# Other margins for places in scratch, a narrower float32r arena and another order of heads in a one-core decoder step

## The chip, the cores and the metric

The kernel runs on 1 core of one Trainium2 chip, as one launch. The metric is the device time of that launch in microseconds (us), the median of several runs. Five engines work side by side: PE (TensorE, the matmuls, with its weight loads as PEld), DVE (VectorE), ACT (ScalarE), POOL (GpSimd) and SP (SyncE, which here issues every DMA). Each takes its instructions in the order in which the program lists them for it, and an instruction that waits holds back what is behind it on its engine.

## The reference, cut to what matters

One decoder layer runs on 16 meta tokens, a prompt of 256 and 8 samples of 4 tokens, 304 columns in all. The width is 2048.

```python
xn = rms_norm(x, norm_mix)
z = xn @ w_in                                  # RWKV columns | retention columns
o_a, S_a = rwkv7_mixer(z_a, z_prev, S_a0, ...) # 16 heads of 64, a scan over tokens
o_b, S_b = retention_mixer(z_b, S_b0, ...)     # 4 heads of 256, chunks of 128
h = x + concatenate([o_a, o_b]) @ w_out
hn = rms_norm(h, norm_ffn)
h = h + (silu(hn @ w_gate) * (hn @ w_up)) @ w_down     # 2048 -> 5632 -> 2048
```

A last RMS norm gives the outputs; the states of both mixers, for the prompt and for each sample, are outputs too. All of it is float32.

## The kernel before, in words

**The weight stream.** Every large product is done with float32r matmuls on split operands: a 128x512 block of weights comes in by DMA (`wr<-big`), ACT casts it to its high part (`wh`), DVE subtracts to get the low part (`wl`), and PE runs three matmuls for each 128x128 piece: high x high, high x low, low x high (`acc<-xh,wh` and so on). `main` (line 712) walks through `steps()`: the input projection `w_in`, then the output projection in two halves, then gate, up and down of the FFN. Five raw blocks and five split ones are in flight (`WR`, `WS`). SP issues the loads of this stream between all other DMAs, in one queue.

**The order of the input projection.** `sequence()` (line 110) reads `ORDER`: `pN` are the three tiles (k, r, v) of a pair of RWKV heads, `rN` the six tiles (q, k, v) of a retention head, `gN` the two gate tiles of a retention head. A tile is 16 steps of three matmuls. The host packs the weights into `big` in the same order.

**The streams beside it.** Each finished tile starts generators: `pair` (a pair's chunked RWKV scan: LoRA products, `inverse`, `units`, `sample`, `pair_out`), `ret` (a retention head), `gate_jobs`, and later `sample_state` and `held_states`, which update the samples' states. A generator yields where it would wait. Their small matmuls go to PE as `mm`, between those of the main stream. After the output projection (`"hs"`), `sample_state` runs for the eight pairs one after the other (`rest_of(self.later)`): each makes `s0n` (128x512) and loads it on SP, makes `bt` (128x128) and clears it on POOL, fills `bt` and `vx` (128x512) on ACT, multiplies `bt` by `vx` on PE, and adds the product to `s0n`, which is then stored.

**The draft.** `body` (line 1956) builds the program twice. The first build is a draft: `Plan` keeps a modelled clock for each engine (`book`, line 377), and `pick` decides by it which stream goes on next. In the draft every scratch tile has a buffer of its own, so nothing waits for a place. The decisions are logged, and the second build repeats them, so the order of each engine's instructions comes from the draft alone.

**Places in scratch.** In the second build all scratch tiles lie in two arenas, one of float32 and one of float32r (`arena_dt.float` and `arena_dt.float32r` in the profile). Their addresses come from `Room`. During the draft `Room.use` (line 532) notes for each tile its size, the numbers of its first and last instruction, the time `at` of its first use and the time `until` at which its last use is done. What counts as the time of first use is set in `book`: PE's present matmul for PE, the engine's own clock less 400 ns for DVE, ACT and POOL, SP's clock less 8000 ns for SP. POOL's clock moves when POOL does something: a clear of a fresh tile starts in the draft as soon as the clear before it is done.

`Room.pack` (line 561) then takes the tiles one by one in a given order, mostly the largest first. Two tiles whose ranges of instructions overlap may not share an address. For any other tile already placed it works out a margin: the later one's `at` less the earlier one's `until`, cut to 0 if negative. A margin of 2000 ns or more doesn't count as near. Candidates are the lowest address and the ends of near tiles, in order of address; the one with the largest margin is taken, or the first that reaches `gap`; of equal ones the lowest address stays. `place` tries five orders of tiles and falling values of `gap`, and keeps the packing with the least `lack`, the sum of what each tile's margin falls short of 800 ns. The float32r arena is packed first, within `WIDE` = 4288 elements per partition; the float32 arena gets what is left of `ROOM` = 33008.

In the second build a tile that gets another's place waits, by semaphore, until the instructions on the earlier tile are done. If its first instruction is a load, SP waits; if a clear, POOL; otherwise ACT or DVE.

Of the kernel before, what the change touches and what calls it, by code (L numbers as in the profile page):

```python
# [53 lines left out]
RAHEAD = 2  # L54
RSTART = (-1, -1, 6, 5)
RRANK = (20, 21, 22, 2.5)
ORDER = "p0 p1 p2 r0 p3 p4 r1 g0 p5 p6 g1 p7 r2 g2 g3 r3"


PV = {}  # L60
# [22 lines left out]
KEYS = ((0, META, SEQ, 0), (P, P, NP - P, SEQ), (LASTK, 2 * P, T - 2 * P, SEQ + NP - P))  # L83
RMW = SEQ + NP - P + T - 2 * P
ROOM = 33008
WIDE = 4288
FREE, GAPS, TRIES = 800.0, (2000.0, 1000.0, 500.0, 200.0, 50.0, 0.0), 12


# [20 lines left out]
def sequence():  # L110
# [3 lines left out]
    seq = [("in", i) for i in range(3)]  # L114
    for what in ORDER.split():
        h = int(what[1])
# [206 lines left out]
class Plan:  # L323
# [53 lines left out]
    def book(self, eng, what, a, k):  # L377
        self.count += 1
        if not self.draft:
            return  # L380
        aps = [x for x in (*a, *k.values()) if hasattr(x, "shape")]
        out, ins = aps[0], aps[1:]

        at = 0.0
        boxes = [(x.name, self.box(x), x is out) for x in aps if x.name not in self.outside]
        meet = lambda a, b: a[0] < b[1] and b[0] < a[1] and a[2] < b[3] and b[2] < a[3]
        for name, box, writes in boxes:
            for other, done, by, written in self.uses.get(name, ()):
                if (written or writes) and done + 100 > at and not (by == eng == "PE") and meet(box, other):
                    at = max(at, done + (30 if by == eng else 100 if eng == "PE" else 60))  # L390
        n = math.prod(out.shape[1:])
        if eng == "PE":
            done = self.array(what, *a[:3], at) + 170
        elif eng == "SP":
            self.clock[eng] = at = max(self.clock[eng] + 400, at)
            self.dma = max(self.dma, at + 1400) + 4 * out.shape[0] * n / 320
            done = self.dma + 600
        else:
            each = sum(math.prod(x.shape[1:]) == 1 for x in ins) if n > 1 else 0
            if eng == "DVE":  # L400
                big = max(math.prod(x.shape[1:]) for x in aps)
                per = 0.56 if what == "tensor_scalar" and ins[0].name not in self.banks else 1.05
                dur, tail = {"stream_shuffle": (62 + 1.05 * n, 90), "transpose": (95 + 1.02 * n, 80), "tensor_reduce": (40 + 1.8 * big, 85),
                             "tensor_tensor_scan": (65 + 2.1 * n, 85)}.get(what, (62 + per * n + 67 * each, 83))
            elif eng == "ACT":
                dur, tail = 108 + 0.83 * n + 90 * each - 40 * (ins[0].name in self.banks), 94
            else:
                dur, tail = (60 + 0.85 * n, 60) if what == "memset" else (125 + 0.8 * n, 65) if what == "tensor_copy" else (185 + 1.65 * n, 60)
            key = (out.start_partition(), ins[0].start_partition() if ins else 0)
            ready = self.clock[eng]  # L410
            if eng != "POOL" and key != self.part[eng]:
                ready += tail + (25 if eng == "ACT" else 31)
                self.part[eng] = key
            self.started = max(ready, at)
            at = self.share(eng, what, ins, self.started, dur, each) + dur
            self.clock[eng] = at
            done = at + tail
        for x in aps:
            for room in self.rooms.values():
                room.use(x, self.count, self.begun if eng == "PE" else self.clock[eng] - (8000 if eng == "SP" else 400), done)  # L420
        for name in {x.name for x in aps if x.name in self.left}:
            self.left[name] -= 1
            assert self.left[name] >= 0, name
            if not self.left[name]:
                self.free[self.at.pop(name)] = done
        for name, box, writes in boxes:
            uses = self.uses.setdefault(name, [])
            if writes:
                uses[:] = [u for u in uses if not (box[0] <= u[0][0] and u[0][1] <= box[1] and box[2] <= u[0][2]
                                                   and u[0][3] <= box[3])]  # L430
            uses.append((box, done, eng, writes))
        self.end = max(self.end, done + 100)
# [87 lines left out]
class Room:  # L520
# [40 lines left out]
    def pack(self, order, limit, gap):  # L561
        done, places, lack, end = [], [0] * len(self.spans), 0.0, 0
        for i in order:
            size, a, b, at, until = self.spans[i]
            size = -(-size // 8) * 8
            near = []
            for o, n, c, d, s, u in done:
                if a <= d and c <= b:
                    near.append((o, o + n, -1.0))
                else:  # L570
                    free = max(0.0, at - u if d < a else s - until)
                    if free < 2000.0:
                        near.append((o, o + n, free))
            near.sort()
            best = None
            for o in sorted({0, *(e for _, e, _ in near)}):
                if o + size > limit:
                    break
                free = min((f for s, e, f in near if s < o + size and o < e), default=2000.0)
                if free > -1.0 and (best is None or free > best[0]):  # L580
                    best = free, o
                    if free >= gap:
                        break
            if best is None:
                return i
            lack += max(0.0, FREE - best[0])
            places[i] = best[1]
            end = max(end, best[1] + size)
            done.append((best[1], size, a, b, at, until))
        return lack, end, places  # L590
# [1365 lines left out]
def body(tc, I, O):  # L1956
# [5 lines left out]
    Step(tile.TileContext(nc[0]).__enter__(), nc[1], nc[2], ExitStack(), rooms, True, log).build(gam4)  # L1962
    rooms[F32R].place(WIDE)
    rooms[F32].place(ROOM - rooms[F32R].size)
# [24 lines left out]
```

## Time and profile before

| | us |
|---|---|
| median of 3 runs | 1529.55 (1529.4 to 1532.66) |
| the profiled execution | 1529.31 |
| its span, first to last instruction | 1527.4 |
| PE busy | 1496.6 |
| weight loads busy | 1474.8 |
| DVE busy | 1086.4 |
| ACT busy | 884.1 |
| POOL busy | 30.6 |

The profile is of one execution. A line of the timeline has the start and the length of an instruction (several alike are merged, with their count), its engine, its operation, and the tiles as out<-in; in brackets stands how long the engine was idle before it, and who ended that wait. A line of the waits has the sum, the number and the longest. `acc` are the accumulators of the main stream, `mm` the other banks. All scratch tiles appear under the two arenas' names, so a tile is recognized by its shape, its operation and its place in time. Nearly all instructions carry one line number, that of the helper which records them (L318). In time the span divides thus: the input projection up to about 549 us, the output projection from 572, the FFN from some 686 to 1515.

### The profile page before, as it was taken

What the parts mean: (1) busy time and instruction counts of PE and PEld (TensorE: products, weight loads), DVE (VectorE), ACT (ScalarE), POOL (GpSimd) and SP (SyncE); (2) the same over time, 40 slices, a digit from 0 to 9 for tenths busy, and PEclk for the clock granted to TensorE, in tenths of its full rate; (3) what the DMA queues carried; (4) which work ended last, traced back from release to release, by engine and by line L of the source; (5) the groups of instructions that cost most, each with busy time, mean ns of one, the idle gap of its engine ahead of it and who ended that gap; (6) DMA issues with size and microseconds to landing.
All of it is one profiled execution on the core that took longest, in us unless ns stands there. A gap on an engine that the chain in (4) does not pass through costs nothing.

```text
span 1527.4 us, 31997 instructions
## 1 busy us (share of the span) xinstructions
PE 1496.6 (98%) x11438; PEld 1474.8 (97%) x11438; DVE 1086.4 (71%) x2768; ACT 884.1 (58%) x2109; POOL 30.6 (2%) x165
## 2 busy tenths in 40 slices
PE   8999999999999999999999999999999999999997
PEld 8999899999999989998899999999999999999997
DVE  6989888998999758775565656556565656565657
ACT  6786668887876875566644444444444444444445
POOL 1000000000000000000000000000000000000000
PEclk9999999999999999999999999999999999999999
DMA  7654443554444358865665655565655555555563
GB/s 236 178 139 145 157 150 114 172 165 136 128 130 132 103 188 263 301 173 176 210 174 171 173 167 172 169 176 167 173 167 172 173 172 168 173 170 171 171 174 123
DMA packets 138783, 258.57 MB, mean 169 GB/s; under 512 B 16256, under 2 KB 22656, under 8 KB 138624
## 3 DMA queue, kind: packets, MB, share of 16 engines
q1 hardware_dynamic: 138624, 256.52, 55.9%
q8 instruction: 91, 1.49, 0.4%
q14 instruction: 68, 0.56, 0.1%
HBM read 242.18 MB, written 14.28 MB: 168 GB/s over the span
## 4 chain that ended last, share of the span: by engine, by line
PE 92%; DVE 3%; ACT 2%; DMA 1%; issue 1%; SPq 0%; DVEq 0%; ACTq 0%
PE acc L318 82%; PE mm L318 11%; DVE arena_dt.float L318 2%; ACT arena_dt.float L318 1%; DVE wl L318 1%; DMA wr<-big 1%; ACT wh L318 0%; DMA arena_dt.float<-xT 0%; SPq L318 0%; DMA arena_dt.float<-s0r 0%; DVE arena_dt.float32r L318 0%; ACT arena_dt.float32r L318 0%; DVE xl L318 0%; DMA arena_dt.float<-lora 0%; ACT xh L318 0%
## 5 line engine op out<-in xcount | busy, mean ns | idle before, releaser
L318 PE MATMUL acc<-xh,wh 128*128 128x288 f32 (+2 forms) x2592 | 781.7, 302 | 1.2 <-ACT wh L318 1.2
L318 PE MATMUL acc<-xh,wl 128*128 128x288 f32 (+2 forms) x2592 | 764.1, 295 | 0.4 <-DVE wl L318 0.3
L318 PE MATMUL acc<-xl,wh 128*128 128x288 f32 (+2 forms) x2592 | 761.0, 294 | 0.0
L318 ACT CAST wh<-wr 128x512 fp32r<-128x512 f32 (+1 forms) x827 | 504.8, 616 | 355.2 <-PE acc L318 306.0
L318 DVE TENSOR_TENSOR wl<-wr,wh 128x512 fp32r<-128x512 f32 (+1 forms) x827 | 559.6, 685 | 129.8 <-ACT wh L318 126.4
L318 PEld LDWEIGHTS acc<-xh,wh 128*128 128x128 f32 x2592 | 487.2, 188 | 5.9 <-issue 3.6
L318 PEld LDWEIGHTS acc<-xl,wh 128*128 128x128 f32 x2592 | 486.7, 188 | 3.0 <-issue 1.9
L318 PEld LDWEIGHTS acc<-xh,wl 128*128 128x128 f32 x2592 | 485.7, 187 | 1.3 <-DVE wl L318 0.9
L318 PE MATMUL acc<-arena_dt.float32r,wh 128*128 128x288 f32 x1408 | 273.0, 292 | 0.2 <-DVE arena_dt.float L318 0.2
L318 PEld LDWEIGHTS acc<-arena_dt.float32r,wh 128*128 128x128 f32 x1408 | 223.8, 188 | 0.6 <-DVE arena_dt.float L318 0.4
L318 PE MATMUL acc<-arena_dt.float32r,wl 128*128 128x288 f32 x704 | 205.7, 292 | 0.0
L318 DVE TENSOR_TENSOR arena_dt.float<-acc,arena_dt.float 128x288 f32<-128x288 f32 (+4 forms) x181 | 72.7, 419 | 149.9 <-PE acc L318 147.1
L318 PE MATMUL mm<-arena_dt.float 128*128 128x128 f32 (+6 forms) x1120 | 164.0, 300 | 15.3 <-issue 9.0
L318 DVE TENSOR_TENSOR arena_dt.float<-arena_dt.float 128x32 f32<-128x32 f32 (+22 forms) x658 | 159.9, 279 | 14.2 <-ACT arena_dt.float L318 8.8
L318 PEld LDWEIGHTS mm<-arena_dt.float 128*128 128x128 f32 (+1 forms) x1120 | 138.8, 182 | 25.2 <-issue 13.7
L318 DVE TENSOR_TENSOR arena_dt.float<-arena_dt.float,acc 128x288 f32<-128x288 f32 (+1 forms) x210 | 94.5, 451 | 85.9 <-PE acc L318 82.0
L318 ACT ACTIVATE arena_dt.float<-arena_dt.float 128x288 f32<-128x288 f32 (+7 forms) x229 | 97.2, 432 | 99.3 <-DVE arena_dt.float L318 96.9
L318 PEld LDWEIGHTS acc<-arena_dt.float32r,wl 128*128 128x128 f32 x704 | 132.2, 188 | 0.0
L318 ACT COPY arena_dt.float<-mm 64x64 f32<-64x64 f32 (+10 forms) x338 | 94.8, 289 | 59.0 <-PE mm L318 50.6
L318 ACT COPY arena_dt.float<-arena_dt.float 128x32 f32<-128x32 f32 (+8 forms) x267 | 62.3, 283 | 26.1 <-DVE arena_dt.float L318 22.1
L318 ACT CAST arena_dt.float32r<-arena_dt.float 128x288 fp32r<-128x288 f32 (+6 forms) x117 | 49.4, 429 | 48.4 <-DVE arena_dt.float L318 40.2
L318 DVE TENSOR_TENSOR arena_dt.float32r<-arena_dt.float,arena_dt.float32r 128x288 fp32r<-128x288 f32 (+6 forms) x116 | 52.1, 452 | 18.5 <-ACT arena_dt.float32r L318 18.1
(68 smaller groups left out, 573.3 us busy)
## 6 DMA issues: line engine op xcount, KB each, us to landing
wr<-big SPq DMA_DIRECT2D x823, 256.0 KB, 2.8
arena_dt.float<-s0r SPq DMA_DIRECT2D x24, 512.0 KB, 5.6
out_rts<-arena_dt.float SPq DMA_DIRECT2D x16, 512.0 KB, 4.3
arena_dt.float<-s0w SPq DMA_DIRECT2D x16, 256.0 KB, 2.9
arena_dt.float<-xT SPq DMA_DIRECT2D x4, 576.0 KB, 6.3
arena_dt.float<-lora SPq DMA_DIRECT2D x16, 128.0 KB, 2.5
out_rws<-arena_dt.float SPq DMA_DIRECT2D x8, 256.0 KB, 3.2
out_y<-arena_dt.float SPq DMA_DIRECT2D x7, 288.0 KB, 2.4
```

The lines of the kernel that those rows point to most:

```text
L318: return self._plan.keep(f(*a, **k))
```

## The change

`ORDER` is another: `g0` comes right after `r0` (before: after `r1`), and `p7` comes before `g1` (before: after it). `WIDE` is 3792 (before 4288). The first use of a tile by SP counts from SP's clock less 3000 ns (before 8000), the first use by POOL from PE's clock (before: POOL's own, less 400 ns). Margins are no longer cut at 0: negative ones are kept, two tiles that may not share have a margin of minus infinity, and any other place can be chosen, with the largest margin first as before.

```diff
-ORDER = "p0 p1 p2 r0 p3 p4 r1 g0 p5 p6 g1 p7 r2 g2 g3 r3"
+ORDER = "p0 p1 p2 r0 g0 p3 p4 r1 p5 p6 p7 g1 r2 g2 g3 r3"
...
-WIDE = 4288
+WIDE = 3792
...
-                room.use(x, self.count, self.begun if eng == "PE" else self.clock[eng] - (8000 if eng == "SP" else 400), done)
+                room.use(x, self.count, self.begun if eng == "PE" else self.clock["PE"] if eng == "POOL" else self.clock[eng] - (3000 if eng == "SP" else 400), done)
...
                 if a <= d and c <= b:
-                    near.append((o, o + n, -1.0))
+                    near.append((o, o + n, -math.inf))
                 else:
-                    free = max(0.0, at - u if d < a else s - until)
+                    free = at - u if d < a else s - until
                     if free < 2000.0:
                         near.append((o, o + n, free))
...
-                if free > -1.0 and (best is None or free > best[0]):
+                if free > -math.inf and (best is None or free > best[0]):
```

## The prediction

> **What bounds the kernel now.** I read the page first, then the windows by stage, then the waits and the timeline around every idle stretch of TensorE. The page's head:
>
> ```profile
> span 1527.4 us, 31997 instructions
> PE 1496.6 (98%) x11438; PEld 1474.8 (97%) x11438; DVE 1086.4 (71%) x2768; ACT 884.1 (58%) x2109; POOL 30.6 (2%) x165
> ```
>
> The matmuls fill 98% of the span, and none is removed or added. So only 1527.4 − 1496.6 = 30.8 us are open, and those at the start and the end lie outside the change. The windows say where the rest is (columns: length, busy time and count of PE, weight load, DVE, ACT, POOL; then clock, DMA share, GB/s):
>
> ```profile
> 20.00:150.00 130.00, 130.00 (x971) 129.07 (x970) 112.99 (x347) 96.99 (x277) 0.76 (x2) 1.00 0.54 162
> 150.00:196.00 46.00, 43.41 (x322) 39.77 (x321) 40.21 (x183) 30.75 (x84) 1.70 (x13) 1.00 0.46 145
> 196.00:205.00 9.00, 6.23 (x38) 5.99 (x37) 7.36 (x21) 5.01 (x15) 0.52 (x1) 0.81 0.63 193
> ...
> 273.00:403.00 130.00, 127.88 (x983) 124.97 (x983) 118.81 (x397) 104.44 (x314) 9.25 (x48) 1.00 0.49 150
> 403.00:500.00 97.00, 96.15 (x750) 95.95 (x749) 90.80 (x389) 68.47 (x202) 4.63 (x25) 1.00 0.47 133
> ...
> 555.00:565.00 10.00, 8.69 (x68) 6.27 (x69) 5.01 (x14) 6.74 (x20) 0.58 (x1) 1.00 0.68 252
> ...
> 605.00:616.00 11.00, 9.26 (x71) 8.95 (x70) 6.46 (x14) 4.59 (x9) 0.00 (x0) 1.00 1.02 353
> ...
> 705.00:745.00 40.00, 34.62 (x242) 31.90 (x241) 20.80 (x36) 26.02 (x84) 0.61 (x3) 1.00 0.63 205
> 745.00:1490.00 745.00, 745.00 (x5778) 744.52 (x5777) 445.90 (x805) 326.65 (x564) 0.00 (x0) 1.00 0.59 172
> ```
>
> Length minus PE's busy time: 2.59, 2.77, 2.12, 0.85, 1.31, 1.74 and 5.38 us, 16.8 us in all; from 745 to 1490 there is none. That 16.8 us, with what the clock adds, is the whole room. The question is which of these gaps are waits for a place in scratch.
>
> **The change, part by part.** Three of its four edits (the margins, the two start times, the width) move tiles to other addresses only: the draft that fixes each engine's order gives every tile its own buffer and never sees a place. They cost no instruction. What they can change is who waits for whom. The fourth, the order of heads, moves whole jobs.
>
> *Clears late, at the FFN's start.* DMA issues of the eight pairs' sample states, and what SP waited for between 700 and 760:
>
> ```profile
> 702.63 0.33 SPq L318 DMA_DIRECT2D arena_dt.float<-s0w  x1
> 703.05 2.28 SPq L318 DMA_DIRECT2D wr<-big  x5
> 711.67 0.33 SPq L318 DMA_DIRECT2D arena_dt.float<-s0w  x1
> ...
> 712.59 1.88 SPq L318 DMA_DIRECT2D wr<-big  x4
> 720.33 0.33 SPq L318 DMA_DIRECT2D arena_dt.float<-s0w  x1
> ...
> 721.23 1.89 SPq L318 DMA_DIRECT2D wr<-big  x4
> 730.31 0.33 SPq L318 DMA_DIRECT2D arena_dt.float<-s0w  x1
> ```
> ```profile
> SPq L318 <- PE mm L318: 19.3, 3, 7.2
> ```
> ```profile
> 716.56 0.62 ACT L318 CAST wh<-wr 128x512 fp32r<-128x512 f32 x1 [2.33 <-DMA wr<-big]
> ```
> ```profile
> 719.20 1.10 PE L318 MATMUL mm<-arena_dt.float 128*128 128x512 f32 x2 [1.59 <-issue]
> 729.18 1.10 PE L318 MATMUL mm<-arena_dt.float 128*128 128x512 f32 x2 [1.99 <-issue]
> 738.00 1.10 PE L318 MATMUL mm<-arena_dt.float 128*128 128x512 f32 x2 [1.38 <-issue]
> ```
>
> SP stands still from 705.33 (703.05 + 2.28) to 711.67, from 714.47 to 720.33 and from 723.12 to 730.31: 6.3, 5.9 and 7.2 us, the 19.3 us that it waited for a matmul. The matmul of 719.20 ends at 720.30, and 0.03 us later the next state's load goes out; 729.18 + 1.10 = 730.28 and 730.31 say the same. A load into a fresh tile needs only its place, so each load has the place of an operand of the matmul before, `bt` or `vx`. The weights queue behind that load on SP; the cast of 716.56 waits 2.33 us for them; ACT's work for `vx` is behind that cast; and the next matmul of the kind is late. The loop feeds itself, four times, for 5.38 us.
>
> The code says why. `bt` is cleared by POOL, and the first use of a cleared tile counted from POOL's clock in the draft. A clear of a fresh tile waits for nothing there, so that clock stands far back (POOL is busy 30.6 us of the whole span). Every margin against such a tile came out negative, was cut to 0, and with all margins equal the lowest address won. With PE's clock and no cut, `bt` sees a true margin, and any place unused for 2 us beats the one that the next load wants. At 700 us the pairs are done and scratch has room. I take the whole 5.38 us. Bounds: 0 if load and operand still meet, 5.38 if they don't; near the upper, since one cause explains all four.
>
> The other side of it: a clear may now get a place that comes free only shortly before PE's clock, and the later clears queue behind it on POOL, with whoever reads them.
>
> ```profile
> POOL arena_dt.float L318 <- PE mm L318: 263.9, 11, 112.3
> ```
>
> POOL already waits that long, and none of PE's idle rows here names it; I count nothing, and one gap of 2.77 us (next row) at worst.
>
> *The gap at 200.*
>
> ```profile
> 197.73 0.56 ACT L318 ACTIVATE arena_dt.float<-arena_dt.float,omu 128x312 f32<-128x312 f32 x1 [3.68 <-DVE arena_dt.float32r L318]
> ```
> ```profile
> 199.90 0.79 PE L318 MATMUL mm<-arena_dt.float 128*128 128x128 f32 x2 [2.77 <-ACT arena_dt.float L318]
> ```
> ```profile
> 200.00:202.00 2.00, 2.00 (x9) 2.00 (x10) 1.25 (x4) 1.70 (x6) 0.00 (x0) 0.50 0.29 92
> 202.00:204.00 2.00, 2.00 (x13) 2.00 (x13) 1.29 (x5) 0.62 (x2) 0.00 (x0) 0.76 0.83 168
> 395.00:397.00 2.00, 1.30 (x11) 1.33 (x11) 1.70 (x6) 1.56 (x6) 0.00 (x0) 1.00 1.01 347
> ```
>
> The activation writes `d`, a fresh tile, from `z` and a constant; nothing that it reads comes out of DVE's hi/lo split, so it waited 3.68 us for its place. Behind it on ACT stood the copy and cast that PE needed: 2.77 us idle, and then the clock was granted at 0.50 and 0.76 for two windows of 2 us, (0.50 + 0.24) x 2 = 1.48 us more. Price 4.25 us. After the 2.12 us gap at 395 the clock stayed at 1.00. The Trainium skill, page "TensorE: Matmul & The Clock Gate", Part 1, says that the clock halves after an idle window of about 3.4 us; by it this gap would be too short to cost more than its 2.77 us, and the sum would be 1.5 us smaller; the 0.50 row decides against it. I take 4.25 us as gone: the order of heads changes this neighbourhood, and a negative margin is now avoided while another place is less bad. Bounds 0 and 4.25.
>
> *Loads early: LoRA weights and retention states.*
>
> ```profile
> ACT arena_dt.float32r L318 <- DMA arena_dt.float<-lora: 7.8, 4, 3.0
> ```
> ```profile
> 394.87 0.41 ACT L318 CAST arena_dt.float32r<-arena_dt.float 128x256 fp32r<-128x256 f32 x1 [3.01 <-DMA arena_dt.float<-lora]
> ```
> ```profile
> 160.15 1.08 PE L318 MATMUL mm<-arena_dt.float 128*128 128x64 f32 x8 [0.68 <-issue]
> 178.85 0.46 PE L318 MATMUL mm<-arena_dt.float 128*128 128x128 f32 x2 [0.72 <-ACT arena_dt.float L318]
> 395.69 0.46 PE L318 MATMUL mm<-arena_dt.float 128*128 128x128 f32 x2 [2.12 <-issue]
> 485.17 0.46 PE L318 MATMUL mm<-arena_dt.float 128*128 128x128 f32 x2 [0.85 <-issue]
> 561.99 1.06 PE L318 MATMUL mm<-arena_dt.float 128*32 128x256 f32 x12 [0.73 <-DMA arena_dt.float<-s0r]
> 615.13 0.72 PE L318 MATMUL mm<-arena_dt.float32r 128*128 128x512 f32 x2 [1.74 <-ACT arena_dt.float32r L318]
> ```
>
> Four times ACT stood before a late LoRA load, and each of the first four gaps, 0.68 + 0.72 + 2.12 + 0.85 = 4.37 us, follows one. A place that comes free late would hold the load back; so would plain queueing on SP. Bounds 0 and 4.37; I take half, 2.2, because scratch is full in this stage and the rows don't separate the two. The 1.31 us near 560 wait for state loads: half again, 0.65. The 1.74 us at 615 stay: the DMA share there is 1.02, so bytes are short and not places. The 3000 for 8000 on loads lets a place be up to 5 us younger; the three holds above, 5.9 to 7.2 us each, cost some 1.3 to 2 us of PE, so one such slip costs under 2 us.
>
> *Narrower float32r arena.* 496 elements fewer, a little less than one hi/lo tile (2 x 288 = 576), so a split's cast on ACT may wait for the matmuls that read the tile before. Bounds: a gain where float32 tiles get the 496 elements, or one wait like that at 197.73, 4.25 us.
>
> *Order.* `g0` is 2 tiles x 16 x 3 = 96 matmuls; at 745/5778 = 0.129 us that is 12.4 us, taken from after `r1` to before `p3`; `p7` starts 12.4 us earlier, `g1` one pair later. PE's total stays. The load on DVE moves (below). New waits from width and order together: 0 to two gaps of 4.25; I take one gap of 2.77 us, the nearest row for a wait in this stage.
>
> Sum against the profiled execution (1529.31 us; its span 1527.4 and 1.91 outside): −5.38 − 4.25 − 2.2 − 0.65 + 2.77 = −9.7, so 1519.6. The median of the runs shown is 0.24 above: **1519.9 us**.
>
> **The rivals.**
>
> *Only the FFN's start gains.* Between 150 and 565 scratch is full, and true margins only choose among bad places; for it speaks that gaps of different kinds stand there side by side. 1529.55 − 5.4 = 1524.2 us.
>
> *The places stay as bad.* The packing takes large tiles first and `bt` is among the smallest; if the load still meets it or `vx`, and the p-stage trades gaps one for one, 1529.5 us. Against it: after 700 us little else holds a place.
>
> *DVE becomes the bound.* Slower. Rows for it:
>
> ```profile
> L318 DVE TENSOR_TENSOR wl<-wr,wh 128x512 fp32r<-128x512 f32 (+1 forms) x827 | 559.6, 685 | 129.8 <-ACT wh L318 126.4
> L318 DVE TENSOR_TENSOR arena_dt.float<-acc,arena_dt.float 128x288 f32<-128x288 f32 (+4 forms) x181 | 72.7, 419 | 149.9 <-PE acc L318 147.1
> ```
>
> From 273 to 403, with `g0`, `p5`, `p6`, `g1` and the start of `p7`, DVE is busy 118.81 of 130 us: 11.2 free. A gate's 12.4 us of PE need 8 weight subtractions of 0.685 and some 6 vector instructions of about 0.42, 8.0 us of DVE, and leave 4.4 free. The new order takes both gates out: 11.2 − 8.8 = 2.4 us free in 105, 98% busy. If each of `p5`, `p6`, `p7` then loses one gap like that at 200 and the old gaps stay: 3 x 4.25 − 5.38 = +7.4, 1536.9 us. It decides from two such gaps on (8.5 − 5.4 = +3.1). Against it: from 403 to 500 DVE is 94% busy (90.80 of 97) and PE lost only 0.85 us; and the gates come back at either side.
>
> **How the numbers follow.** About 0.2%, 3.1 us, is what a measurement here can tell from no change. Forecast 0.48, only the FFN 0.24, as bad as before 0.13, DVE 0.15. The first two are faster: 0.72, 0.13, 0.15. Low end: every gap goes that may, that at 615 too, and nothing new: 5.38 + 4.25 + 4.37 + 1.31 + 1.74 = 17.1, so 1512.5; I set 1513. High end: 1531, past no change; that leaves out most of the DVE case and little else.
>
> **What would show it.** Right: in the FFN's first 50 us the sample-state loads go out without a wait for a matmul, and PE has no gap there; no window at half clock before the end; fewer waits of ACT for LoRA loads. The clears on POOL may wait as long as before, since nothing needs them early. Wrong: those gaps still in place, or new gaps of over 2 us between 280 and 400 with DVE at 98%, or an ACT cast that waits for a matmul's operand tile.

## The result, and the profile after

| | us |
|---|---|
| before, median of 4 runs | 1529.55 (1529.4 to 1532.66) |
| after, median of 4 runs | 1509.44 (1509.02 to 1511.9) |
| ratio after / before | 0.9867, 95% interval 0.985 to 0.9884 |
| span of the profiled execution, before and after | 1527.4 and 1507.3 |

The change takes 20.1 us off. The prediction was 1519.9 us with a range from 1513 to 1531: the direction was right, the gain is twice what was forecast, and the time lies below the range. Executions that took over 1.5% longer than the shortest of their kernel are left out of the ratios below; only two of the experiments have any.

The head of the page of the kernel after:

```profile
span 1507.3 us, 31980 instructions
...
PE 1493.5 (99%) x11438; PEld 1475.3 (98%) x11438; DVE 1086.2 (72%) x2768; ACT 884.7 (59%) x2109; POOL 31.9 (2%) x165
```

The same 11438 matmuls. TensorE is busy 3.1 us less (1496.6 − 1493.5) and idle 17.0 us less (30.8 before, 1507.3 − 1493.5 = 13.8 now). The windows of the kernel after by stage, with the columns as in the prediction (length, busy time and count of PE, weight load, DVE, ACT and POOL, then clock, DMA share and GB/s):

```profile
20.00:150.00 130.00, 130.00 (x965) 128.96 (x964) 113.25 (x344) 95.85 (x271) 7.93 (x40) 1.00 0.54 166
150.00:200.00 50.00, 50.00 (x395) 47.82 (x395) 47.26 (x218) 36.80 (x105) 1.87 (x12) 1.00 0.52 164
200.00:273.00 73.00, 72.31 (x554) 71.53 (x553) 63.02 (x178) 62.20 (x185) 5.18 (x25) 1.00 0.41 119
273.00:403.00 130.00, 129.42 (x992) 126.91 (x991) 121.27 (x419) 106.89 (x320) 7.50 (x39) 1.00 0.51 156
403.00:500.00 97.00, 97.00 (x761) 96.89 (x759) 91.31 (x388) 66.64 (x193) 5.80 (x29) 1.00 0.46 131
500.00:555.00 55.00, 55.00 (x431) 52.73 (x430) 34.66 (x85) 44.48 (x125) 1.37 (x3) 1.00 0.61 204
605.00:616.00 11.00, 11.00 (x86) 10.91 (x85) 7.84 (x15) 5.48 (x10) 0.20 (x1) 1.00 0.98 368
700.00:745.00 45.00, 45.00 (x329) 43.07 (x329) 27.98 (x51) 28.03 (x78) 0.41 (x2) 1.00 0.67 208
```

Length minus TensorE's busy time is 0.69 us between 200 and 273, 0.58 between 273 and 403, and 0 in the other rows: 1.27 us where the prediction counted 16.8 before. The clock is 1.00 in every row. What is left of TensorE's gaps between 20 and 1470 us, the two longest:

```profile
299.14 1.13 PE L318 MATMUL mm<-arena_dt.float 128*128 128x128 f32 x8 [0.58 <-ACT arena_dt.float32r L318]
```
```profile
201.03 1.13 PE L318 MATMUL mm<-arena_dt.float 128*128 128x128 f32 x8 [0.25 <-DVE arena_dt.float L318]
```

What SP waited for between 680 and 745 in the kernel after, all that it lists, and four of the loads of the sample states with the weights between them:

```profile
SPq L318 <- DVE wl L318: 44.2, 35, 3.0
SPq L318 <- DVE arena_dt.float L318: 1.1, 1, 1.1
SPq L318 <- PE acc L318: 0.2, 1, 0.2
```
```profile
690.16 0.42 SPq L318 DMA_DIRECT2D arena_dt.float<-s0w  x1
...
691.35 5.56 SPq L318 DMA_DIRECT2D wr<-big  x4
696.96 0.42 SPq L318 DMA_DIRECT2D arena_dt.float<-s0w  x1
...
698.86 6.15 SPq L318 DMA_DIRECT2D wr<-big  x4
705.06 0.42 SPq L318 DMA_DIRECT2D arena_dt.float<-s0w  x1
...
711.75 0.43 SPq L318 DMA_DIRECT2D arena_dt.float<-s0w  x1
```

The 19.3 us that SP stood before a matmul at this place are gone. SP now waits almost only for the weight stream's own buffers (`wl`), 3.0 us at the longest: the stops of 6.3, 5.9 and 7.2 us ahead of a state load have no counterpart. An activation that writes a `d` near 198 in the kernel after; then the largest group of retention state loads, with the load and the DMA share before it, first before, then after:

```profile
197.88 0.55 ACT L318 ACTIVATE arena_dt.float<-arena_dt.float,omu 128x312 f32<-128x312 f32 x1
```
```profile
543.49 0.38 SPq L318 DMA_DIRECT2D arena_dt.float<-rmask  x1
557.35 2.74 SPq L318 DMA_DIRECT2D arena_dt.float<-s0r  x6
```
```profile
500.00:555.00 55.00, 54.85 (x426) 54.29 (x424) 38.96 (x93) 44.63 (x129) 1.76 (x6) 1.00 0.38 108
```
```profile
532.37 0.42 SPq L318 DMA_DIRECT2D arena_dt.float<-rmask  x1
532.89 4.45 SPq L318 DMA_DIRECT2D arena_dt.float<-s0r  x6
```

The activation has no wait in brackets (3.68 us before); the copy ahead of it on ACT does wait there, 2.33 us for a result of DVE, and the gap of TensorE behind it is 0.25 us. The six state loads stood 13.5 us behind the load before them (557.35 − 543.87); now they follow it at once, and the DMA share of 500 to 555 rises from 0.38 to 0.61. ACT's waits list no wait for a LoRA load any more (7.8 us before).

### The profile page after: what moved, and what is told of

Its sections match the earlier page's. It is cut to its first block, busy times and chain, and to the rows that moved or that the text cites. A ratio compares the mean times of both kernels' runs of the same rounds, so it can differ in the third digit from the quotient of the medians.

```text
span 1507.3 us, 31980 instructions
## 1 busy us (share of the span) xinstructions
PE 1493.5 (99%) x11438; PEld 1475.3 (98%) x11438; DVE 1086.2 (72%) x2768; ACT 884.7 (59%) x2109; POOL 31.9 (2%) x165
## 4 chain that ended last, share of the span: by engine, by line
PE 95%; DVE 3%; ACT 1%; issue 0%; DMA 0%; SPq 0%; DVEq 0%; ACTq 0%
PE acc L318 84%; PE mm L318 11%; DVE arena_dt.float L318 2%; ACT arena_dt.float L318 1%; DVE wl L318 1%; DMA arena_dt.float<-xT 0%; SPq L318 0%; ACT wh L318 0%; ACT arena_dt.float32r L318 0%; DVE arena_dt.float32r L318 0%; DVE xl L318 0%; DVEq L1985 0%; ACT xh L318 0%; ACT shout L318 0%; DVEq L318 0%
## 5 line engine op out<-in xcount | busy, mean ns | idle before, releaser
L318 DVE TENSOR_TENSOR arena_dt.float<-arena_dt.float 128x288 f32<-128x288 f32 (+21 forms) x658 | 159.6, 279 | 10.2 <-ACT arena_dt.float L318 7.9
L318 PE MATMUL mm<-arena_dt.float 128*128 128x128 f32 (+7 forms) x1120 | 162.0, 299 | 0.8 <-ACT arena_dt.float32r L318 0.6
L318 ACT COPY arena_dt.float<-mm 64x64 f32<-64x64 f32 (+11 forms) x338 | 95.1, 290 | 43.8 <-PE mm L318 39.7
L318 ACT COPY arena_dt.float<-arena_dt.float 128x8 f32<-128x8 f32 (+8 forms) x267 | 62.4, 283 | 26.7 <-DVE arena_dt.float L318 25.4
```

The costliest lines, as they stand in the source:

```text
L318: return self._plan.keep(f(*a, **k))
```

## The experiments

**The theories.** Mine: the gain is places alone. Tiles that had got a place freed too late held back SP, ACT or POOL; the new order of heads and the narrower arena bring nothing or cost. The first rival: the new order spreads DVE's load, and with it the waits. Later rivals concern which of the packing edits does it, and why the gain is twice the forecast. Each expectation is quoted as it was written before its run; a letter in it names a theory which that text, or the one ahead of it, states. Every ratio is to the kernel before on the same chip, with its 95% interval.

**The new order alone.**

```diff
-ORDER = "p0 p1 p2 r0 p3 p4 r1 g0 p5 p6 g1 p7 r2 g2 g3 r3"
+ORDER = "p0 p1 p2 r0 g0 p3 p4 r1 p5 p6 p7 g1 r2 g2 g3 r3"
```

> The kernel before with the new order of heads alone; margins, start times and width as before. Theory A (the gaps were waits for places, and POOL's clock made the bad places): the FFN's gaps near 700 to 745 us stay, about 5 us with loads of sample states that go out right at the end of a matmul, and the input projection keeps gaps of its own, so 1525 to 1533 us. Theory B (the gaps in the input projection were a crowded DVE, and the order spreads its load): the idle stretches between 150 and 500 us go, some 8 us with the clock, while the FFN's 5.4 us stay: 1519 to 1522 us.

Measured: ratio 1.0016 (1.0 to 1.0032); 1530.73 us is the median of the seven executions in it, 1532.78 that of all ten. Three of its gaps:

```profile
349.71 0.49 PE L318 MATMUL mm<-arena_dt.float 128*128 128x128 f32 x2 [2.13 <-ACT arena_dt.float L318]
```
```profile
578.14 3.85 PE L318 MATMUL mm<-arena_dt.float 128*32 128x256 f32 x18 [2.14 <-DMA arena_dt.float<-s0r]
```
```profile
736.62 1.85 PE L318 MATMUL mm<-arena_dt.float 128*128 128x512 f32 x2 [2.31 <-issue]
```

The gaps are of the old kinds at other times, the FFN's start among them. The order alone gains nothing.

**POOL's time of first use alone, and all but that.** `pool_only` is the kernel before with one edit:

```diff
-... self.clock[eng] - (8000 if eng == "SP" else 400), done)
+... self.clock["PE"] if eng == "POOL" else self.clock[eng] - (8000 if eng == "SP" else 400), done)
```

> The kernel before with one edit: the first use by POOL counts from PE's clock. Order, width, SP's 8000 ns and the cut at 0 as before. Theory A: the FFN's 5.4 us go, and most of the gaps between 150 and 500 with them, since cleared tiles no longer take places blindly: 1514 to 1519 us. Theory B: only the FFN's 5.4 us go: 1523 to 1526 us.

`pool_own` is the kernel after with that one edit undone:

```diff
-... self.clock["PE"] if eng == "POOL" else self.clock[eng] - (3000 if eng == "SP" else 400), done)
+... self.clock[eng] - (3000 if eng == "SP" else 400), done)
```

> The changed kernel with one edit undone: the first use by POOL counts from POOL's own clock less 400 ns again. The new order, the width, SP's 3000 ns and the uncut margins stay. Theory A: the FFN's gaps come back and gaps in the input projection too, 1520 to 1530 us. Theory B: 1512 to 1516 us, since only the FFN's part is lost.

Measured: `pool_only` 1512.56 us, 0.9891 (0.9877 to 0.9906); `pool_own` 1512.1 us, 0.9891 (0.9876 to 0.9906). The first gives most of the gain, about 17 us, more than either theory said. The second was expected by theory A to lose much of it and did not. Its time lies in B's range, but not for B's reason, that the FFN's gaps come back: its timeline lists no gap between 604 and 760. So POOL's clock isn't the only way to mend the bad places. The waits of ACT for LoRA loads, in `pool_only` and, for comparison, in `sp_only` (3000 for 8000 on SP alone, below):

```profile
ACT arena_dt.float32r L318 <- DMA arena_dt.float<-lora: 0.3, 1, 0.3
```
```profile
ACT arena_dt.float32r L318 <- DMA arena_dt.float<-lora: 6.7, 3, 4.3
```

Before it was 7.8 us. So mending POOL's clock clears these waits too, and SP's 3000 ns alone doesn't.

**All packing edits, with the old order and width.** Against the kernel after:

```diff
-ORDER = "p0 p1 p2 r0 g0 p3 p4 r1 p5 p6 p7 g1 r2 g2 g3 r3"
+ORDER = "p0 p1 p2 r0 p3 p4 r1 g0 p5 p6 g1 p7 r2 g2 g3 r3"
-WIDE = 3792
+WIDE = 4288
```

> The kernel before with both start times and the uncut margins of the change, but with the old order and the old width. Theory A: nearly all of the gain, 1509 to 1515 us, with what is missing in loads of states and LoRA weights for which the narrower float32r arena made room. Theory B: the FFN's 5.4 us and little else, 1521 to 1525 us.

Measured: 1507.76 us, 0.986 (0.9844 to 0.9877), and its timeline lists no gap between 20 and 1472 us. Is it better than the kernel after? Both went once more, side by side on one chip.

> The changed kernel once more, beside the next one on one chip, to see what the new order and the narrower float32r arena are worth on top of the packing: 1508 to 1511 us.

> The packing's edits with the old order and the old width once more. Theory A (the packing is all of the gain, and the new order brings gaps of its own near 201, 239 and 299 us, 1.3 us in the changed kernel's trace): 1 to 2 us below the changed kernel. Theory G (the order and the width carry part of the gain): level with it or above by over 1 us.

Measured: 1510.14 us, 0.9877 (0.9862 to 0.9893), for the kernel after, and 1506.98 us, 0.9858 (0.9842 to 0.9875), without the order and the width: 3.2 us less by the medians. The intervals just overlap, but no execution of the one (1506.62 to 1507.39) reaches into those of the other (1507.92 to 1511.18). This is the fastest version of all. The gap near 610 is no firm mark of a program, for this second profile of the same kernel shows it again:

```profile
599.19 0.72 PE L318 MATMUL mm<-arena_dt.float32r 128*128 128x512 f32 x2 [1.16 <-ACT arena_dt.float32r L318]
```

**Single tiles moved.** To price each kind of wait by itself, the kernel before kept all its edits undone, and after `place` a few float32 tiles were put elsewhere: of all addresses where a tile meets no other in its lifetime, the one whose other users are farthest away, counted in instructions.

```diff
+    def move(self, limit, starts):
...
+                near = [a - d if d < a else c - b if b < c else -1 ...]
+                free = min(near, default=1 << 30)
+                if free >= 0 and (best is None or free > best[0]):
+                    best = free, o
+            self.places[i] = best[1]
...
+    rooms[F32].move(ROOM - rooms[F32R].size, (("bt_", 0),))
```

The last line is that of `mv_bt` (the eight `bt`); `mv_d` names one tile `d`, `mv_lw` the sixteen LoRA loads, `mv_late` two `s0r` and two `ht` between 540 and 565.

> The kernel before, with only the eight bt tiles of the sample states given other places (those that are longest unused, all else at its old address). Theory A (the state's load met the operand bt of the matmul before): the loads near 700 to 740 us go out without a wait for a matmul, PE's four gaps there go, 5.4 us, and the earlier gaps stay: 1523 to 1525.5 us. Rival C (the weights come late there for want of bytes or of SP's time, whatever the places): the gaps stay, 1528 to 1531 us.

> The kernel before, with one single tile moved: the d tile that the activation at 197.7 us writes. Theory A: that activation no longer waits 3.7 us, the gap of 2.77 us before 200 goes, and with it the half clock after it: 4.25 us, 1524.5 to 1526.5 us. Rival D (PE waits there for DVE's work, which the released activation doesn't hasten): a gap of about 2 us stays near 200, 1528 to 1530 us.

> The kernel before, with only the sixteen tiles of the LoRA loads moved to places longest unused. Theory A (these loads waited for places): ACT's four waits for LoRA loads, 7.8 us, nearly go, and the gaps of 0.68, 0.72, 2.12 and 0.85 us with them: 4.4 us, 1524.5 to 1526.5 us. Rival E (they waited in SP's queue behind the weights): the waits stay, 1528 to 1531 us. The prediction's half would be 1527.3 us.

> The kernel before, with only four loads moved: the two retention states and the two residual blocks that are loaded between 540 and 565 us. Theory A' (SP stands before these places, and the states, which the queue holds back, then crowd the DMA at 600): SP's hold from 543.9 to 557.4 us shrinks, the gaps near 560 (1.31 us) and at 615 (1.74 us) go: 1526 to 1527.5 us. Rival F, as predicted (bytes are short at 615): the gap at 615 stays at over 1 us, 1528 to 1530 us.

| moved | median, us | ratio (95%) | less, us |
|---|---|---|---|
| 8 `bt` | 1523.18 | 0.9964 (0.995 to 0.9979) | 6.4 |
| 1 `d` | 1525.79 | 0.9983 (0.9971 to 0.9994) | 3.8 |
| 16 LoRA loads | 1524.76 | 0.9964 (0.9948 to 0.9979) | 4.8 |
| 2 `s0r`, 2 `ht` | 1526.84 | 0.9987 (0.9978 to 0.9997) | 2.7 |

(Last column: 1529.56, the median before on that chip, less the median.) What SP waited for between 700 and 760 with `bt` moved; the activation for `d` with that tile moved; the state loads with those moved:

```profile
SPq L318 <- DVE wl L318: 39.4, 32, 3.0
SPq L318 <- DVE arena_dt.float L318: 1.1, 1, 1.1
SPq L318 <- PE acc L318: 0.4, 1, 0.4
```
```profile
193.79 0.55 ACT L318 ACTIVATE arena_dt.float<-arena_dt.float,omu 128x312 f32<-128x312 f32 x1
```
```profile
547.01 5.11 SPq L318 DMA_DIRECT2D arena_dt.float<-s0r  x6
```

In each run the gaps of its own kind are gone and the others stay, though not at the same size: the gap at 615, 1.74 us before, is 0.38 to 0.79 in all four, whatever was moved. With `bt` moved, SP's wait for the matmul is no longer listed. With `d` moved, ACT doesn't wait there. With the LoRA loads moved, all four gaps behind them are gone. With the state loads moved, the six go out at 547.01 and not at 557.35, and TensorE doesn't wait for them. The four sum to 17.7 us by the medians (by the ratios 15.6; each interval is some 2 us to either side), most of the 20.1, and scratch had a better place for each of the 29 tiles all along.

**All 29 together.** The edit is the four lists in one.

> The kernel before, with the four groups of tiles moved together (bt, the one d, the LoRA loads, the four late loads), 29 tiles of 958, all other edits left out. Theory A (the gaps are separate waits for places and add up): 6.4 + 3.8 + 4.8 + 2.7 = 17.7 us less, 1511 to 1514 us. Rival L (one wait taken away only uncovers the next): under 12 us less, over 1517 us.

Measured: 1536.56 us, 1.0047 (1.003 to 1.0064): slower than before, where some 1511 was due. Its gaps between 20 and 1490 sum to only 1.99 us. What it lost came from elsewhere, as in the next run.

**Uncut margins alone.**

```diff
-                    near.append((o, o + n, -1.0))
+                    near.append((o, o + n, -math.inf))
...
-                    free = max(0.0, at - u if d < a else s - until)
+                    free = at - u if d < a else s - until
...
-                if free > -1.0 and (best is None or free > best[0]):
+                if free > -math.inf and (best is None or free > best[0]):
```

> The kernel before with the uncut margins alone; POOL's own clock, SP's 8000 ns, order and width as before. Theory H (POOL's clock and the cut did harm only together: with either mended, a blind choice ends): FFN's gaps go, 1512 to 1518 us in all. Theory I (margins taken from the wrong clock go on choosing wrong places, and the runs of the changed kernel with POOL's own clock were saved by the order and by SP's 3000 ns): 1520 to 1528 us.

> The kernel with the uncut margins alone once more, because in all of its executions so far each FFN matmul took 0.133 us instead of 0.129, which two other kernels show in some of their executions and not in others. Theory H (either mending ends the blind choice): no gap near 700 to 745 us, about 7 us of gaps in all before 620, 1514 to 1519 us with matmuls at 0.129. Theory K (the slow matmuls belong to these addresses): 1544 to 1547 us again, in every execution.

Measured, on two chips: 1545.94 us, 1.0113 (1.0098 to 1.0128), and 1546.75 us, 1.0114 (1.0097 to 1.0132), outside both ranges of the first expectation. One window in the middle of the FFN, first of the kernel with uncut margins, then of the kernel before:

```profile
800.00:1000.00 200.00, 200.00 (x1502) 200.00 (x1501) 116.34 (x211) 84.56 (x147) 0.00 (x0) 1.00 0.56 164
```
```profile
800.00:1000.00 200.00, 200.00 (x1554) 200.00 (x1553) 119.54 (x217) 87.76 (x152) 0.00 (x0) 1.00 0.58 171
```

TensorE is full in both, the clock is 1.00 in both, but 1502 matmuls went through in place of 1554: one each 0.1332 us, against 0.1287. That lasts for some 5780 matmuls, from about 740 us to 1507, and costs 5780 x 0.0045 = 26 us. The edit itself does mend places: the FFN's start has no gap in this kernel, and 1546.3 − 26 = 1520, an estimate, is where it would stand. `mv_all` shows the same: 1502 matmuls in the same window, and 1536.56 − 26 = 1510.6.

**The loads' time alone, and the pairs.** `sp_only` is the kernel before with 3000 for 8000; `nocut_sp` adds the uncut margins; `pool_sp` has 3000 and POOL's edit with margins still cut.

```diff
-... (8000 if eng == "SP" else 400), done)
+... (3000 if eng == "SP" else 400), done)
```

> The kernel before with SP's 3000 ns for 8000 ns alone; POOL's own clock and the cut as before. Theory A: cleared tiles are still placed blindly, so part of the gaps stays, the FFN's among them: 1521 to 1528 us. Theory J (the 8000 ns were what hid good places from the loads): 1512 to 1516 us.

> Uncut margins and SP's 3000 ns together, POOL's own clock, old order and width: what the changed kernel with POOL's own clock had, without its order and width. Theory H: 1512 to 1517 us, so the order and the width weren't what saved it. Theory I (they were): over 1520 us.

> PE's clock for POOL and SP's 3000 ns, margins still cut at 0, old order and width. It shares out the 4 us between POOL's clock alone (1512.6 us) and the whole packing (1507.8 us). Theory M (the cut costs the rest: loads that can't have a good place still take the lowest address): 1510 to 1513 us. Theory N (the 3000 ns bring the rest): 1507 to 1509 us.

Measured: `sp_only` 0.9968 (0.9957 to 0.9979), 1523.82 us as the median of the six executions in it; the other three of nine took about 1549, and the profile, which is of one of those, has the 0.133 us too. `nocut_sp` 1515.1 us, 0.9913 (0.9891 to 0.9935). `pool_sp` 1509.08 us, 0.9871 (0.9851 to 0.9891). So the uncut margins with the loads' time reach most of the gain with POOL's own clock, the old order and the old width; and POOL's edit with the loads' time reaches all of it with the margins still cut. POOL's clock and the cut did harm together. Mending the clock alone takes 17 us off, mending the cut alone some 9 by the estimate above.

**Nine small matmuls in the FFN.** Why 0.133 us? Two theories stood at the end: the program (through its addresses) has that rhythm, or each small matmul that breaks the stream sets the rhythm anew until the next. The last small matmul runs at about 740; after it comes the long stretch. The edit, made to the kernel with uncut margins and to `pack_w4288`, adds a product that nobody reads:

```diff
+            if k == 0 and key[0] == "gate" and key[1] >= 8 and key[1] % 4 == 0:
+                self.pe.matmul(self.ps(1)[:, :6 * key[1]], hi[:, o:o + m], xh[:, :6 * key[1]], start=True, stop=True)
             self.pe.matmul(acc[:m, :n], hi[:, o:o + m], xh, start=k == 0, stop=False)
```

> The kernel before with uncut margins, and nine added matmuls (48 to 240 columns, their product unused), one ahead of every fourth gate tile from the ninth on. In the profiles so far the FFN's stream runs in one of two rhythms, 386 or 400 ns for each three matmuls, and changes between them only where another matmul stands between. Theory L (each such break chooses the rhythm anew, and it holds until the next break): stretches of both kinds between the nine, so less than the 1546 of nocut_only, between 1523 and 1545. Theory P (the rhythm belongs to the program, to where its instructions or tiles lie): all at 400 ns as before, about 1547 to 1549.

> pack_w4288 (all packing edits, old order and width), with the same nine added matmuls. Theory L: some of the stretches between them go over to 400 ns for three matmuls, so slower than the 1507 of pack_w4288 by more than the nine matmuls themselves (about 0.1 us each): 1511 to 1533. Theory P: 386 ns throughout, 1508 to 1509. If both kernels keep their rhythm from end to end, L falls.

Measured: 1541.19 us, 1.0081 (1.0064 to 1.0098), and 1517.2 us, 0.992 (0.9905 to 0.9934). Windows of 65 us, each between two of the added matmuls, first with uncut margins, then `pack_w4288`:

```profile
820.00:885.00 65.00, 65.00 (x490) 65.00 (x489) 38.63 (x70) 27.48 (x48) 0.00 (x0) 1.00 0.53 165
895.00:960.00 65.00, 65.00 (x506) 65.00 (x506) 38.62 (x71) 28.45 (x50) 0.00 (x0) 1.00 0.57 173
970.00:1035.00 65.00, 65.00 (x490) 65.00 (x489) 37.59 (x68) 26.85 (x47) 0.00 (x0) 1.00 0.55 166
```
```profile
805.00:870.00 65.00, 65.00 (x506) 65.00 (x506) 39.50 (x72) 28.90 (x50) 0.00 (x0) 1.00 0.57 168
880.00:945.00 65.00, 65.00 (x489) 65.00 (x489) 38.16 (x70) 27.75 (x49) 0.00 (x0) 1.00 0.54 163
955.00:1020.00 65.00, 65.00 (x507) 65.00 (x506) 39.24 (x72) 28.42 (x49) 0.00 (x0) 1.00 0.56 169
```

The count goes 490, 506, 490 in one kernel and 506, 489, 507 in the other, and it changes only at an added matmul. Of the ten stretches that nine matmuls make, two of the one kernel run at 0.129 us and three of the other at 0.133. The times agree: from one added matmul to the next it is 76.9 us at the one rhythm and 74.4 at the other, 2.5 us; two stretches are 5 us, and the ratio fell from 1.0114 to 1.0081, 5.0 us; three are 7.6 us beside the added matmuls, and the ratio rose from 0.986 to 0.992, 9.2 us. So a program has no one rhythm: it can change where the stream is broken, and then holds.

## Why the prediction was wrong

**What held.** The waits are waits for places, they are the ones that the prediction named, and the sign is right. The FFN's start was put at 5.38 us: `mv_bt` measured 6.4 and SP's wait is gone, so the loop of state load, weights, cast and matmul is shown. The gap at 200 with its clock was put at 4.25 us (1.48 of it the clock; 9 us at 0.81 make 1.7): `mv_d` measured 3.8. In its profiled execution the clock fell after another gap instead, which in the profile before had left it at 1.00:

```profile
391.23 0.46 PE L318 MATMUL mm<-arena_dt.float 128*128 128x128 f32 x2 [1.99 <-issue]
```
```profile
391.00:398.00 7.00, 6.77 (x39) 6.80 (x40) 6.59 (x20) 5.62 (x20) 0.00 (x0) 0.76 0.62 200
```

The Trainium skill, page "TensorE: Matmul & The Clock Gate", Part 1, has the clock halve after an idle window of about 3.4 us; by it neither this gap nor that of 2.77 us would have cost more than itself, and the traces disagree.

**Where it failed.** Three steps.

1. *LoRA loads, half of 4.37 us, "because scratch is full in this stage and the rows don't separate the two".* `mv_lw` measured 4.8 us (5.5 by the ratio), with all four gaps gone by addresses alone. Scratch had room: each of the 16 tiles found a place, with every other tile where it was, for which ACT no longer waits. I had taken the packing's outcome for a lack of room, and sized the term at less than half. Nor had I said which edit would free them: I named POOL's clock for `bt` alone, but `pool_only` leaves 0.3 of the 7.8 us that ACT waited for these loads, and `sp_only` 6.7.
2. *State loads, half of 1.31 us.* With them moved, both gaps near 560 are gone, so the whole 1.31 was a wait for places; `mv_late` measured 2.7 us (2.0 by the ratio, 0.5 to 3.4). *The 1.74 at 615 "stay".* This gap is gone in the kernel after, but why stays open. It was 0.38 to 0.79 us in the four runs with moved tiles, three of which moved no state load, and none or 1.16 us in two profiles of `pack_w4288`. The DMA share of 1.02 doesn't settle it either: it is 0.98 in the kernel after, with no gap.
3. *One new wait of 2.77 us for width and order.* TensorE's remaining gaps sum to about 1.3 us; `pack_w4288` has none of them between 200 and 300, so they come with the order or the width, at under half the price. The total effect of those two edits is a loss, 3.2 us by the pair on one chip; where the rest of it lies is not settled.

With the measured terms in place of mine, 6.4 + 3.8 + 4.8 + 2.7 = 17.7 less 1.3, the sum is 16.4 us, 1513.1. What lacks to 1509.4 is no more than the four intervals leave open together (some 4 us, adding in squares). The profiles show part of it: short gaps in the input projection that the prediction didn't price, 0.63 and 0.53 us among them, and 0.9 us at the start, where TensorE is busy 16.12 of the first 20 us before and 17.04 after. That last one is chance: in a second profile of the kernel after it is 15.37.

**The explanation of the cause** was right but too narrow. It named POOL's clock together with the cut at 0, and that clock for `bt` at the FFN's start alone. `pool_only`, which takes 17 us off and leaves two gaps between 20 and 760, of 1.55 and 0.87 us, shows that the clock was behind nearly all the late places. And the two need not go together: `nocut_sp` gets some 13 us by its ratio with POOL's clock as it was. My reading is that a wrong margin does less harm while it still ranks places; no run shows that by itself.

**The rivals.** "Only the FFN's start gains" and "as bad as before" fell with the first windows. "DVE becomes the bound" fell too: between 273 and 403 DVE is busy 121.27 of 130 us, 2.5 more than before, and TensorE lost 0.58 us. DVE at 93% over that window left TensorE fed.

**The range.** Its low end took the forecast's gaps as all that could go, 17.1 us, and was set at 1513. Left out of it were the small gaps and the rest of TensorE's busy time: of the 3.1 us less the clock is 1.7, and 1.4 was in no term; what it is, no run shows.

## What to carry to other kernels

Here a static packer that cut its margins and took the time of first use from an idle engine's modelled clock handed out places freed too late, and the price was not paid by the tile but by what queued behind its wait: at the FFN's start, the weight stream on SP. Before putting a row of gaps down to lack of room or of bandwidth, move the tiles and look; four of the waits here read as waits for a DMA and were waits for a place. And compare windows of the undisturbed stretches too, by their counts of matmuls: `mv_all`, with hardly a gap left, lost all its gain in a rhythm that no gap shows.

## What the runs showed of the hardware that was not expected

**Two rhythms of a full TensorE.** The FFN's stream, three matmuls of 288 columns for each piece of weight, goes at 386 or at 400 ns for three, with TensorE busy throughout and the clock at 1.00. The rhythm holds for hundreds of microseconds, and every change seen stands where another matmul or a short wait breaks the stream. Late in the FFN it is a wait: in `nocut_only` the slower rhythm ends at 1508, beside a gap of 0.16 us, and in the kernel after the faster one ends at 1472, beside one of 0.15. In the two runs with added matmuls, those of 72, 96 and 216 columns changed it in both, that of 192 in one, those of 48, 120, 144, 168 and 240 in neither; why, no run shows. In `nocut_only` (two chips) and `mv_all` every execution fell into the slower one; of `order_only` and `sp_only` three of ten and three of nine took 25 to 29 us more than the median of the others, as they would by it (a profile shows it for `sp_only` alone). The kernels before and after and `pack_w4288` show no such time in any execution, and the comparison of before and after is free of it up to 1470 us.

**The clock after short gaps.** In `pool_only` a gap of 1.55 us was enough to bring the clock down (the second fence has the windows' columns):

```profile
168.40 1.10 PE L318 MATMUL mm<-arena_dt.float 128*128 128x64 f32 x8 [1.55 <-ACT arena_dt.float L318]
```
```profile
168.00:175.00 7.00, 6.60 (x45) 5.75 (x45) 5.27 (x24) 4.81 (x12) 0.26 (x2) 0.76 0.16 51
```

At 0.76 over 7 us that is 7 x 0.24 = 1.7 us of TensorE's time, as much again as the gap. In `nocut_only` a longer gap left it at 1.00, as the 2.12 us at 395 did before; in `nocut_kick` a gap of nearly the same length, at the same matmul, brought it down:

```profile
198.59 0.49 PE L318 MATMUL mm<-arena_dt.float 128*128 128x128 f32 x2 [2.27 <-ACT arena_dt.float L318]
```
```profile
196.00:206.00 10.00, 7.73 (x60) 7.38 (x59) 8.20 (x32) 7.90 (x24) 0.00 (x0) 1.00 0.70 240
```
```profile
196.50 0.80 PE L318 MATMUL mm<-arena_dt.float 128*128 128x128 f32 x2 [2.25 <-ACT arena_dt.float L318]
```
```profile
194.00:204.00 10.00, 7.75 (x50) 7.51 (x50) 7.41 (x30) 6.76 (x20) 0.00 (x0) 0.83 0.64 226
```

Length alone doesn't decide it. What does, no run shows.
